# Which earlier readings an attention score group waits for, in a one-core hybrid decoder layer

## The chip, the core and the metric

The kernel runs on one core of a Trainium2 chip. The core has a matmul engine (PE, with its weight loads shown apart as PEld), a vector engine (DVE), a scalar engine (ACT), GpSimd (POOL), a queue engine that here mostly issues transfers (SP), and 16 DMA engines. Each engine carries out its own list of instructions in order; between engines they wait on semaphores. The metric is the device time of one launch in microseconds (us), lower is better. PE's clock is granted by a throttle; the profile gives it as a share of full speed.

## The reference

One decoder layer on x (1 x 2048 x 1024), float32. What matters here:

```
hn = rms_norm(h, mix_pre_g)
proj = hn @ w_in                      # q, k, v for attention and u for the convolution group
attn_out = sliding_window_attention(q, k, v, attn_sinks, rel_bias)
conv_out = conformer_conv(u, ...)     # GLU, causal depthwise conv of width 31, layer norm, swish, pointwise
mixed = concat([attn_out, conv_out]) @ w_out
h = h + rms_norm(mixed, mix_post_g)
hn = rms_norm(h, ffn_pre_g)
ff = (silu(hn @ w_gate) * (hn @ w_up)) @ w_down
h = h + rms_norm(ff, ffn_post_g)
```

Attention has 8 query heads of 64 in two groups that share a key and a value head each. In blocks of 128 queries, each query sees its own block of keys and the one before, inside a window of 128, with a bias by distance and one learned sink per head:

```
s = einsum("bnqhgd,bnkhd->bnhgqk", qb, kb) * scale
s = where(valid, s + bias, -inf)
m = maximum(max(s), sink);  p = exp(s - m)
p = p / (sum(p) + exp(sink - m))
o = einsum("bnhgqk,bnkhd->bnqhgd", p, vb)
```

The feed-forward width is 2816.

## The kernel before

**Stages.** The sequence is cut into four token tiles of 512 (t = 0 to 3). Every product is float32 in two parts, high and low, and so three matmuls; nearly all matmuls are issued by one helper (line 108 of the profile), so rows are told apart by tile names, whose letter after the @ is the stage. Stage A is the input projection of a tile (GLU units, then keys, values and queries), B its attention, C its convolution group (480 tap operations on DVE for the four tiles, `fc@C` at L85 in the profile, then transposes into the bank `ct`), W the output projection, H builds the operands of the feed-forward product (the layer uses sums and differences of them), F is gate and up, G the down projection. J joins the convolution group's pointwise product with the output projection; X is preparation.

**Interleaving.** Stages are Python generators. A main stage runs and "lanes" with other stages are pumped beside it by a model of the time that has gone by: B, C and W0 beside A, C and H0 and the rest of B beside W1 and the first part of F, C, W and H of the later tiles beside G. The instructions so emitted go to a scheduler (a tile framework with a timeline model, L1558), which sets every engine's final order by priority and by when it reckons an instruction ready. An added dependency can therefore change the order of all engines.

**PSUM banks.** There are eight: four `mm`, three `tr`, one `ct`. Attention works in the `tr` banks.

**Attention (stage_b).** It works on four blocks of 128 queries a tile. `front(b)` computes a block's scores in two groups. A group takes two `tr` banks and fills them with 12 matmuls, alternating between the banks (`tr@B<-kz,ql@A` in the profile). The matmuls after a group's first get a very high priority, so that a group is issued in one piece once its first is. DVE reads each bank: it masks (L469) and then, per head, adds the bias and takes the maximum while it writes the scores out (L472). The last reading of each bank is recorded in a list by `freed`: two entries per group. After both groups ACT takes the exponentials (L492). `back(b)` scales, transposes the probabilities of four heads into one `tr` bank (L514), copies them out on ACT (L515, recorded by `freed`), has GpSimd select the part that belongs to the block before (L517), twice; then eight matmuls (four in the first block of all) form the weighted sums in a `tr` bank (`tr@B<-p@B,vd@B` and `tr@B<-p@B,vtok`), ACT copies them to `at` (L544, recorded by `freed`), and a transfer on ACT's queue writes them to `mixT` in DRAM (L546). The order of emission in a tile is front 0, front 1, back 0, front 2, back 1, front 3, back 2, back 3.

**The order around a score group.** The first matmul of a group is tied by explicit, synchronizing dependencies to two entries of `freed`'s list: the third-last and the second-last. With three banks handed out in turn these are the last uses of the two banks that the group overwrites; the last entry is the use of the bank that it doesn't touch.

**Neighbours that the prediction speaks of.** Keys `kz` and values `vtok` are single buffers per tile. W0's and W1's operands are loaded from `mixT` on SP's queue (L765; `fa@W`, and `mb@J` for W1's first load), split by ACT (L754) and DVE, and multiplied into `mm` banks. The next piece of the convolution is loaded on SP's queue (L603, `fc@C<-y_scr`) and transposed at L575. H0 transposes columns into the one bank `ct` (L863); ACT scales them out into one of two `gb` buffers (L883), a transfer on ACT's queue stores these (L884).

Of the kernel before, what the change touches and what calls it, by code (L numbers as in the profile page):

```python
# [37 lines left out]
def layer_kernel(ctx, tc, x, xT, cols, rows, sinks, relb, onehot, w_in, w_pw, w_out, w_gate, w_up, w_down, out):  # L38
# [19 lines left out]
    def f4(tag, shape=(P, D)):  # L58
        return t_(tag, shape)
# [7 lines left out]
    def sm(n, dt=F32):  # L67
        kind = "A" if lab[0][0] == "G" else lab[0][0]
        return sb.tile([P, 8], dt, tag="sm" + kind, name=nm("sm"), bufs={"C": 8, "W": 4}.get(kind, 16))[:, 0:n]
# [37 lines left out]
    def mat(*args, **kw):  # L107
        r = nc.tensor.matmul(*args, **kw)  # L108
        if not inlane[0]:
            lead_pe[0] = r  # L110
        return r
# [68 lines left out]
    def after_first(first, r, how=mybir.DependencyClass.NoSync):  # L180
        tc.add_manual_dep(
            r.ins,
            first.ins.name,
            mybir.DependencyInfo(how, mybir.DependencyReason.DATA),
            reason="order",
        )
# [244 lines left out]
    done_ = []  # L431

    def stage_b(t):
# [3 lines left out]
        def freed(r):  # L437
            done_.append(r)

        def front(b):  # L440
            lab[0] = L
            first = t == 0 and b == 0
            tok = slice(b * P, (b + 1) * P)
            win = slice(b * P, b * P + 256)
            mx = sm(8)
            pr = f4("p", (P, 8, P))
            for ip in range(2):
                os = [tr().rearrange("p (j k) -> p j k", j=2) for _ in range(2)]
                lead = []
                pq = tc.cur_priority  # L450
                for j in range(2):
                    i = 2 * ip + j
                    for n, (a, k) in enumerate(((0, 0), (0, 1), (1, 0))):
                        for g in (1, 0):
                            sl = slice(64 * g, 64 * g + 64)
                            if lead:
                                tc.cur_priority = pq - 10000
                            r = mat(os[g][:, j], q[i][sl, a, tok], kz[sl, k, win], start=n == 0, stop=n == 2)
                            if lead:
                                after_first(lead[-1], r)  # L460
                            else:
                                for x_ in done_[-3:][:2]:
                                    after_first(x_, r, mybir.DependencyClass.Sync)
                            if len(lead) < 2:
                                lead.append(r)
                tc.cur_priority = pq + 1
                for g in range(2):
                    prev = neg.unsqueeze(2).to_broadcast([P, 2, P]) if first else os[g][:, :, 0:P]
                    nc.vector.copy_predicated(os[g][:, :, P:], upper.unsqueeze(1).to_broadcast([P, 2, P]), prev)  # L469
                    for j in range(2):  # L470
                        h = 4 * g + 2 * ip + j
                        read = nc.vector.tensor_tensor_reduce(  # L472
                            out=pr[:, h],
                            in0=os[g][:, j, P:],
                            in1=bias[0][:, h],
                            op0=ALU.add,
                            op1=ALU.max,
                            scale=1.0,
                            scalar=NEG,
                            accum_out=mx[:, h : h + 1],  # L480
                        )
                    freed(read)
                yield 1.3
                lab[0] = L
            negm = sm(8)
            stt(negm, mx, -1.0, nsnk, ALU.mult, ALU.min)
            es = sm(8)
            vtt(es, negm, snk, ALU.add)
            act(es, es, AF.Exp)
            den = sm(8)  # L490
            for h in range(8):
                act(pr[:, h], pr[:, h], AF.Exp, bias=negm[:, h : h + 1], accum_out=den[:, h : h + 1])  # L492
            vtt(den, den, es, ALU.add)
            rd = sm(8)
            nc.vector.reciprocal(rd, den)
            live[b] = pr, rd
            yield YC
# [54 lines left out]
        for b in range(5):  # L552
            if b < 4:
                yield from front(b)
            else:
                yield YC
            if b:
                yield from back(b - 1)
# [1004 lines left out]
```

## Time and profile before

| | us |
| --- | --- |
| median of three runs | 1950.12 (1946.66 to 1955.75) |
| the profiled execution's own time | 1951.89 |
| its span in the trace | 1950.2 |
| PE busy | 1903.6 (98%) |
| DVE busy | 1488.7 (76%) |
| ACT busy | 969.9 (50%) |
| POOL busy | 296.2 (15%) |
| mean granted clock of PE | 0.992 |

The span runs from the first to the last instruction of one profiled execution. A row of a timeline gives start, duration, engine, line, tiles, shapes and a count, and in square brackets the idle time ahead of it with what ended that; a row of the chain gives start and share of the time for which that step set the end; a row of waits gives total, number and longest.

### The profile page before, as it was taken

What the parts mean: (1) busy time and instruction counts of PE and PEld (TensorE: products, weight loads), DVE (VectorE), ACT (ScalarE), POOL (GpSimd) and SP (SyncE); (2) the same over time, 40 slices, a digit from 0 to 9 for tenths busy, and PEclk for the clock granted to TensorE, in tenths of its full rate; (3) what the DMA queues carried; (4) which work ended last, traced back from release to release, by engine and by line L of the source; (5) the groups of instructions that cost most, each with busy time, mean ns of one, the idle gap of its engine ahead of it and who ended that gap; (6) DMA issues with size and microseconds to landing.
All of it is one profiled execution on the core that took longest, in us unless ns stands there. A gap on an engine that the chain in (4) does not pass through costs nothing.

```text
span 1950.2 us, 26810 instructions
## 1 busy us (share of the span) xinstructions
PE 1903.6 (98%) x8730; PEld 1538.2 (79%) x8730; DVE 1488.7 (76%) x2707; ACT 969.9 (50%) x1910; POOL 296.2 (15%) x367
## 2 busy tenths in 40 slices
PE   9999999999899999999999999999999999999998
PEld 7877776777678878878878878877888888888886
DVE  5999899897775899888669985778766675455557
ACT  5356344657567533333364556576543433345443
POOL 6000101221012100000000010015332332311000
PEclk9999999999999999999999999999999999999999
DMA  8897646669668676877487688689644442375654
GB/s 317 276 320 236 224 158 195 195 217 342 226 221 276 231 240 220 265 258 259 134 306 247 216 295 276 203 310 352 226 153 165 162 157 97 130 249 184 215 190 156
DMA packets 229180, 443.55 MB, mean 227 GB/s; under 512 B 22920, under 2 KB 48688, under 8 KB 229040
## 3 DMA queue, kind: packets, MB, share of 16 engines
q1 hardware_dynamic: 207408, 406.19, 62.1%
q10 hardware_dynamic: 19392, 28.32, 4.0%
q0 software_dynamic: 2240, 7.34, 1.0%
q8 instruction: 68, 1.11, 0.2%
q14 instruction: 72, 0.59, 0.1%
HBM read 320.64 MB, written 121.12 MB: 227 GB/s over the span
## 4 chain that ended last, share of the span: by engine, by line
PE 65%; DVE 16%; DMA 12%; issue 3%; ACT 2%; POOL 2%; SPq 1%; DVEq 0%; ACTq 0%; POOLq 0%
PE mm@F L108 29%; PE mm@G L108 17%; PE mm@A L108 9%; DVE fc@C L85 5%; PE mm@W L108 4%; PE tr@W L108 2%; PE tr@B L108 2%; DMA raw@A<-w_in 2%; DVE w@F L85 2%; DVE mid@W L85 1%; PE ct@J L108 1%; DMA mixT<-fc@C 1%; DMA td<-fc@G 1%; DVE chl@F L85 1%; DVE hl@G L85 1%
## 5 line engine op out<-in xcount | busy, mean ns | idle before, releaser
L85 DVE SCALAR_TENSOR_TENSOR fc@C<-glu@C,colt,fc@C 128x512 f32<-128x512 f32 x480 | 353.4, 751 | 2.2
L108 PE MATMUL mm@F<-hl@H,w@F 128*128 128x512 f32 x1056 | 254.8, 390 | 0.3 <-ACT gb@F L1098 0.3
L108 PE MATMUL mm@G<-hl@G,hl@G 128*128 128x512 f32 x924 | 226.3, 395 | 4.6 <-DVE p@G L1225 1.7
L108 PEld LDWEIGHTS mm@F<-hl@H,w@F 128*128 128x128 f32 x1056 | 197.9, 188 | 41.7 <-ACT gb@F L1098 0.7
L108 PEld LDWEIGHTS mm@G<-hl@G,hl@G 128*128 128x128 f32 x924 | 172.3, 189 | 43.8 <-DVE hl@G L85 2.8
L108 PE MATMUL mm@A<-hl@A,w@A 128*128 128x512 f32 x840 | 204.0, 394 | 2.3 <-DVE hl@A L85 1.0
L108 PE MATMUL mm@G<-w@G,hl@G 128*128 128x512 f32 x876 | 199.5, 389 | 0.0
L845 ACT ACTIVATE w@F<-chl@F 128x512 fp32r<-128x512 f32 x220 | 135.3, 624 | 124.3 <-PE mm@F L108 114.2
L108 PEld LDWEIGHTS mm@G<-w@G,hl@G 128*128 128x128 f32 x876 | 164.5, 188 | 34.1
L108 PEld LDWEIGHTS mm@A<-hl@A,w@A 128*128 128x128 f32 x840 | 155.7, 188 | 40.5 <-issue 2.5
L85 DVE TENSOR_TENSOR w@F<-chl@F,w@F 128x512 fp32r<-128x512 f32 x198 | 144.7, 734 | 38.4 <-ACT w@F L845 38.2
L108 PE MATMUL mm@F<-mid@H,w@F 128*128 128x512 f32 x528 | 131.2, 391 | 2.1 <-ACT fa@F L1108 2.1
L108 PE MATMUL mm@F<-ql@H,w@F 128*128 128x512 f32 x528 | 130.8, 391 | 1.5 <-ACT w@F L845 1.5
L108 PE MATMUL mm@F<-p@H,w@F 128*128 128x512 f32 x528 | 129.1, 389 | 0.6 <-ACT at@F L1101 0.6
L108 PE MATMUL mm@F<-x@H,w@F 128*128 128x512 f32 x528 | 128.6, 391 | 0.1
L108 PEld LDWEIGHTS mm@F<-mid@H,w@F 128*128 128x128 f32 x528 | 99.2, 188 | 23.2 <-ACT fa@F L1108 2.5
L108 PEld LDWEIGHTS mm@F<-ql@H,w@F 128*128 128x128 f32 x528 | 98.7, 188 | 22.7 <-ACT w@F L845 1.9
L108 PEld LDWEIGHTS mm@F<-x@H,w@F 128*128 128x128 f32 x528 | 98.5, 188 | 22.4 <-issue 0.8
L108 PEld LDWEIGHTS mm@F<-p@H,w@F 128*128 128x128 f32 x528 | 99.0, 188 | 21.6 <-ACT at@F L1101 1.2
L133 ACT ACTIVATE w@A<-raw@A 128x512 fp32r<-128x512 f32 x110 | 67.5, 626 | 79.5 <-PE mm@A L108 46.1
L85 DVE TENSOR_TENSOR w@G<-raw@G,w@G 128x512 fp32r<-128x512 f32 x73 | 50.8, 696 | 68.5 <-ACT w@G L845 62.5
L108 PE MATMUL mm@W<-w@W,hl@W 128*128 128x512 f32 x384 | 99.9, 407 | 1.8 <-ACT hl@W L754 1.7
(308 smaller groups left out, 3253.9 us busy)
## 6 DMA issues: line engine op xcount, KB each, us to landing
mids<-fa@F SPq DMA_DIRECT2D x154, 256.0 KB, 2.6
raw@A<-w_in SPq DMA_DIRECT2D x55, 512.0 KB, 4.8
w@A<-lo_in SPq DMA_DIRECT2D x84, 256.0 KB, 3.7
fc@G<-mids SPq DMA_DIRECT2D x77, 256.0 KB, 3.4
fa@G<-mids SPq DMA_DIRECT2D x75, 256.0 KB, 5.1
w@W<-lo_out SPq DMA_DIRECT2D x48, 256.0 KB, 4.9
chl@F<-w_gate SPq DMA_DIRECT2D x22, 512.0 KB, 4.5
raw@F<-w_gate SPq DMA_DIRECT2D x22, 512.0 KB, 3.6
```

The lines of the kernel that those rows point to most:

```text
L85: r = op(*args, **kw)
L108: r = nc.tensor.matmul(*args, **kw)
L133: act(w[:, 0], raw, AF.Copy)
L845: act(w[:, 0], x, AF.Copy)
```

## The change

The first matmul of a score group is tied to the two latest entries of the list in place of the third- and second-last. Behind another score group these are the last readings of both of that group's banks. Behind a `back` they are the copy of the second transposes (L515) and the copy of the weighted sums (L544). The hazards of the banks themselves are kept by the framework in either case. No instruction of computation is added or taken away.

```
                             if lead:
                                 after_first(lead[-1], r)
                             else:
-                                for x_ in done_[-3:][:2]:
+                                for x_ in done_[-2:]:
                                     after_first(x_, r, mybir.DependencyClass.Sync)
                             if len(lead) < 2:
                                 lead.append(r)
```

More of the change, by code (lines that the diff above doesn't have):

```diff
@@ L461, in front @@
                             else:
-                                for x_ in done_[-3:][:2]:
+                                for x_ in done_[-2:]:
                                     after_first(x_, r, mybir.DependencyClass.Sync)
```

## The prediction

> **What bounds the kernel now.** I began with the page's busy shares, then read the chain that ended last in order of time.
>
> ```profile
> span 1950.2 us, 26810 instructions
> PE 1903.6 (98%) x8730; PEld 1538.2 (79%) x8730; DVE 1488.7 (76%) x2707; ACT 969.9 (50%) x1910; POOL 296.2 (15%) x367
> ```
>
> ```profile
> 1736.41 196.53 PE mm@G L108 x867
> ```
>
> The matmul engine is busy 98% of the span, and the last chain has stretches such as 867 matmuls back to back, 196.53 / 867 = 0.227 us each. The change touches no instruction, only the order, so this work stays. What can move is the 1950.2 − 1903.6 = 46.6 us in which PE is idle, and the stretches in which it was granted half its clock.
>
> Third, PE's waits in the whole span. The columns are total, times, longest:
>
> ```profile
> PE ct@H L863 <- ACT gb@H L883: 5.1, 3, 3.3
> PE tr@B L108 <- DVE sm@B L472: 3.2, 2, 2.9
> PE tr@B L108 <- POOL p@B L517: 2.8, 1, 2.8
> PE ct@C L575 <- DMA fc@C<-y_scr: 1.8, 1, 1.8
> PE mm@W L108 <- ACT hl@W L754: 1.7, 2, 1.3
> ```
>
> The second row is the score groups' own wait (for the readings at L472): 3.2 us of 1950. The instructions' timelines put nearly all of the first, second and fifth rows at two places, which I call spot 1 and spot 2. Spot 1, first PE's and SP's rows, then the chain:
>
> ```profile
> 324.24 0.97 PE L108 MATMUL tr@B<-kz,ql@A 64*128 64x256 f32 x12
> 332.40 1.55 PE L108 MATMUL tr@B<-kz,ql@A 64*128 64x256 f32 x12 [2.85 <-DVE sm@B L472]
> 335.23 0.80 PE L108 MATMUL mm@W<-w@W,hl@W 128*128 128x512 f32 x1 [1.28 <-ACT hl@W L754]
> ```
>
> ```profile
> 324.41 4.69 DMA mixT<-at@B
> 329.11 0.32 SPq L765
> 329.96 4.57 DMA fa@W<-mixT
> 334.55 0.64 ACT hl@W L754
> ```
>
> A block's second score group (332.40) waits for the readings of its first (324.24), which on DVE lie behind a run of convolution taps. Then W0's first matmul (335.23) waits for operands whose load sits on SP's queue behind W1's first load, and that one waits for the write of B1's last weighted sums (324.41 + 4.69 = 329.10). Spot 2, rows of PE, of ACT and of the chain:
>
> ```profile
> 519.18 0.97 PE L108 MATMUL tr@B<-kz,ql@A 64*128 64x256 f32 x12 [0.39 <-DVE sm@B L472]
> 524.05 1.11 PE L863 MATMUL ct@H<-ident,fa@H 128*128 128x128 f32 x4 [3.32 <-ACT gb@H L883]
> 523.32 0.69 ACT L883 ACTIVATE gb@H<-ct@H,colt 128x512 f32<-128x512 f32 x1 [4.21 <-DMA hT<-gb@H]
> 516.50 6.71 DMA hT<-gb@H
> ```
>
> H0's turned columns (L863) share the single bank ct; its reader at L883 writes one of two gb buffers and so waits for the 6.71 us write of the buffer two columns before. Last, stretches: length, busy of PE, PEld, DVE, ACT and POOL, granted clock, DMA share, GB/s:
>
> ```profile
> 325.00:345.00 20.00, 15.87 (x71) 12.59 (x70) 20.00 (x55) 6.33 (x11) 1.08 (x2) 0.83 0.68 212
> 332.50:339.40 6.90, 5.62 (x22) 4.46 (x23) 6.90 (x14) 1.83 (x4) 0.54 (x1) 0.51 0.87 277
> 345.00:393.00 48.00, 48.00 (x255) 37.71 (x254) 39.73 (x98) 30.44 (x75) 11.87 (x23) 1.00 0.65 201
> 500.00:526.00 26.00, 20.12 (x112) 14.74 (x111) 18.77 (x49) 14.83 (x38) 0.77 (x2) 0.96 0.72 233
> 523.70:530.50 6.80, 6.01 (x16) 4.54 (x17) 4.51 (x16) 5.29 (x16) 0.64 (x1) 0.50 0.48 152
> 526.00:576.00 50.00, 49.95 (x237) 37.10 (x237) 43.08 (x100) 34.59 (x85) 10.90 (x18) 0.95 0.52 174
> ```
>
> After each of the two long waits PE ran some 6.8 us at half its clock: 0.51 after spot 1's 2.85 us, 0.50 after spot 2's 3.32 us.
>
> **The added wait itself.** The first matmul of every score group now waits for the two latest readings of score banks instead of the last uses of just its own two banks; everything behind it in PE's order waits too. How late those readings are, from rows of PE, DVE and ACT:
>
> ```profile
> 180.95 0.97 PE L108 MATMUL tr@B<-kz,ql@A 64*128 64x256 f32 x12
> 176.57 0.09 DVE L472 DVE_READ_ACCUMULATOR2_ANT sm@B<- 128x1 f32 x1
> 114.84 0.97 PE L108 MATMUL tr@B<-kz,ql@A 64*128 64x256 f32 x12 [0.83 <-DVE sm@A L85]
> 114.19 0.07 DVE L472 DVE_READ_ACCUMULATOR2_ANT sm@B<- 128x1 f32 x1
> 114.62 0.07 DVE L472 DVE_READ_ACCUMULATOR2_ANT sm@B<- 128x1 f32 x1
> 165.12 0.97 PE L108 MATMUL tr@B<-kz,ql@A 64*128 64x256 f32 x12
> 166.13 0.58 ACT L544 ACTIVATE at@B<-tr@B 128x512 f32<-128x512 f32 x1
> ```
>
> Behind another score group the readings are long over: 4.3 us at 180.95, the common case. Only at 114.84 does the second bank's reading end 0.43 us after the first's (114.62 against 114.19), so +0.4 us there; a like group in B3 now stands close behind its forerunner, for which I take +1.1 us (0 to 2.85, the row at 332.40 being the longest such wait).
>
> Behind weighted sums it is different: at 165.12 the group started before the copy of the sums (166.13 to 166.71) had run, and in the old order at least eight groups stand directly behind the sums. Kept in that order the new wait would cost each up to 166.71 − 165.12 = 1.6 us, some 13 us in all. But the scheduler reorders: in the new order of PE's instructions 4 to 22 other matmuls stand between the sums and the group, 0.9 to 5 us at 0.227 us each. That is more than the copy's start and 0.58 us need after the sums' last matmul, about 0.7 us, so I cost it at 0; if projection matmuls were missing there, the price is the 13 us above. So much for the wait; what is left is the reordering, which runs over stages A, B, C, W and H of all token tiles.
>
> **Spot 1.** In the new order that second group stands 12.3 us of PE work behind its first instead of 4.1, and on SP's queue four of W0's loads (and a weight load) stand ahead of W1's first load. Both waits, 2.85 + 1.28 = 4.1 us, and the lost clock, (1 − 0.83) × 20.00 = 3.4 us, can go: 7.5 us. Late next is the load of the convolution's next piece, whose wait is the fourth row of PE's waits; the chain there:
>
> ```profile
> 392.50 0.61 DVE fc@C L85
> 393.50 5.11 DMA fc@C<-y_scr
> ```
>
> DVE's work ahead of that piece is only 1.1 us less in the new order. But from 345 to 393 DVE was idle 48.00 − 39.73 = 8.3 us, so it is no hard stop. Between 0 (DVE paces) and 7.5 I take a gain of half, 3.7, as the traced wait is neither gone nor the full bound.
>
> **Spot 2.** The waits are 5.1 (all three at ct are here), 0.39, and the other wait for hl@W, 1.7 − 1.28 = 0.4, which is W1's here: 5.9 us. The clock lost is (1 − 0.96) × 26.00 + (1 − 0.95) × 50.00 = 3.5 us. Together 9.4. In the new order the first column comes 5 us earlier and the score groups are spread between the other columns; the pitch set by two gb buffers and a 6.71 us write stays, so of 5.1 us about 3.3 us of waits should remain, in pieces too short to halve the clock. That frees 9.4 − 3.3 = 6.1 us; as the columns' readiness is a guess, I take two thirds, 4.1, between 0 and 9.4.
>
> [...]
>
> **The late part.** From 1120 to 1340 us (W2, W3 and H2 beside stage G and the next F) the order changes too. The waits that show there:
>
> ```profile
> PE mm@G L108 <- DVE p@G L1225: 1.7, 1, 1.7
> PE tr@H L863 <- issue: 1.5, 1, 1.5
> PE mm@G L108 <- DVE x@G L85: 1.4, 1, 1.4
> ```
>
> At best 4.6 us go, at worst as much comes; nothing says which, so 0, with ±4.6 for the range. Stages F and the end of G keep their order: 0.
>
> **The sum.** −3.7 − 4.1 + 0.4 + 1.1 = −6.3 us. The profiled execution took 1951.89 us (1.7 us outside its span), 1.8 above the median of 1950.12; so 1950.12 − 6.3 = 1943.8, called 1944.
>
> **The rivals.**
> No gain: PE reaches the next limit sooner and waits there. For it speak the wait at L575 and DVE's 20.00 busy of 20.00 us around spot 1; against it the 8.3 us that DVE idles before 393. Sum: +1.5 − 1.5, about 1950.
>
> Slower: a late GpSimd select. At two places the new order leaves fewer matmuls between a block's transposes and its weighted sums: 2.7 us of PE work instead of 6.6 in B1's second block, 3.6 instead of 6.1 at B1's end. The sums read what GpSimd selects at L517. The rows of POOL, DVE and PE where this already bit:
>
> ```profile
> 205.58 8.36 POOL L517 TENSOR_SCALAR_AFFINE_SELECT p@B<-p@B 128x512 f32<-128x512 f32 x2 [15.84 <-ACT p@B L515]
> 203.49 9.36 DVE L85 SCALAR_TENSOR_TENSOR fc@C<-glu@C,colt,fc@C 128x512 f32<-128x512 f32 x14
> 213.99 1.08 PE L108 MATMUL tr@B<-p@B,vd@B 128*64 128x512 f32 x4 [2.77 <-POOL p@B L517]
> ```
>
> Two selects took 8.36 us while a run of taps lasted on DVE, and PE waited 2.77 us. With 2.7 and 3.6 us of cover the same two selects would leave waits of 5.7 and 4.8 us, each with some 3.4 us of half clock behind it as after spot 1: 17 us, minus the 6.3: 1950 + 11 = 1961. [...] But DVE has gaps at most places (39.73 of 48.00 busy), and the 2.77 us wait was not followed by half clock, which speaks for a lower price.
>
> Both spots gone and nothing new: −7.5 − 9.4 + 1.5 = −15.4, about 1935; against it stands the gb pitch.
>
> **How the numbers follow.** Forecast 0.44 (own range 1938 to 1949: the spots at a third or at nearly full), no gain 0.22, late select 0.24, both spots gone 0.10. One measurement tells about 0.5%, 9.75 us, from no change (the three runs spread 9 us). Faster than 1940.4: all of the last case and a third of the forecast's, 0.24. Slower than 1959.9: most of the late selects and a little of no gain, 0.24. The rest 0.52. The range runs from the last case less part of the late stretch, 1933, to the late selects with one more microsecond, 1962; the tails outside, mainly several late selects or a lost cover behind the sums (+13), are about 2 in 10.
>
> **What would show it.** In the changed profile: PE's wait for sm@B at L472 falls from 3.2 us to 1.5 or less, mm@W's wait for hl@W from 1.7 towards 0, ct@H's wait for gb@H from 5.1 to about 3; no half clock around 330 and 525 us, so a mean clock above the 0.992 of before. No gain would show as a longer wait of ct@C for fc@C<-y_scr; the late select as waits of tr@B for p@B at L517 of 4 us or more. Waits of score matmuls for at@B at L544 would break the step on cover.

## The result and the profile after

The changed kernel took 1970.49 us (median of 6 runs, 1963.37 to 1977.87), the kernel before 1950.96 us in the same comparison: a ratio of 1.0096, 95% interval 1.0079 to 1.0113. It is slower by about 19 us, against a forecast of 6.3 us less. The profiled execution took 1970.99 us. Its page, first lines:

```profile
span 1969.3 us, 26817 instructions
PE 1910.3 (97%) x8730; PEld 1539.8 (78%) x8730; DVE 1486.7 (75%) x2707; ACT 972.5 (49%) x1912; POOL 299.4 (15%) x367
```

The number of matmuls is the same; the span grew by 19.1 us. PE's idle time grew from 46.6 to 59.0 us, and the same matmuls were busy for 6.7 us longer. The mean granted clock, 0.991 after 0.992, accounts for 2 to 3 us of these 6.7; where the rest comes from the record does not show. The longest of PE's waits in the changed kernel's whole span, and those that the prediction named (total, times, longest):

```profile
PE tr@W L108 <- DVE mid@W L85: 4.2, 1, 4.2
PE mm@F L108 <- ACT w@F L845: 3.7, 1, 3.7
PE tr@W L108 <- ACT ql@W L754: 3.6, 2, 3.1
PE tr@B L108 <- POOL p@B L517: 3.4, 2, 2.6
PE mm@G L108 <- ACT hl@G L845: 3.2, 1, 3.2
PE mm@A L108 <- DVE x@W L85: 3.2, 1, 3.2
PE mm@F L108 <- DVE fa@F L85: 2.9, 1, 2.9
PE mm@W L108 <- DVE ql@A L85: 2.4, 1, 2.4
PE tr@H L863 <- issue: 2.1, 1, 2.1
PE ct@C L575 <- DMA fc@C<-y_scr: 1.7, 2, 1.2
PE mm@W L108 <- ACT hl@W L754: 1.6, 2, 0.9
PE mm@F L108 <- ACT mm@F L999: 1.4, 1, 1.4
PE ct@H L863 <- ACT gb@H L883: 0.8, 1, 0.8
```

Two of the rows that the prediction wanted gone are gone or small: the score groups' wait for their readings (3.2 us before) is no longer there, ct's for gb went from 5.1 to 0.8. The third, mm@W's wait for hl@W, hardly moved: 1.6 us after 1.7. No wait of score matmuls for at@B (L544) has appeared. The clock at the two spots is whole again, as the stretches of the changed kernel show (length, busy of PE, PEld, DVE, ACT, POOL, granted clock, DMA share, GB/s):

```profile
325.00:345.00 20.00, 18.15 (x95) 13.38 (x94) 19.74 (x34) 10.10 (x19) 5.38 (x5) 1.00 0.85 277
500.00:526.00 26.00, 25.38 (x146) 18.92 (x145) 23.43 (x60) 14.66 (x37) 1.47 (x2) 1.00 0.68 224
526.00:576.00 50.00, 48.83 (x247) 37.07 (x248) 45.58 (x108) 34.41 (x81) 8.39 (x16) 1.00 0.63 211
1226.00:1246.00 20.00, 15.78 (x57) 12.46 (x56) 9.10 (x15) 6.80 (x12) 1.72 (x1) 0.83 0.84 268
```

But six waits of 1.4 to 4.2 us stand there that before did not have, and they have nothing to do with score groups: W0's sums on DVE at 385 us (x@W), a query split at 485 (ql@A), a reading and a sum of F at 578 and 657 (L999, fa@F), and in the late part W3 (mid@W) and G (hl@G). The last stretch quoted, with 15.78 of 20.00 us busy at a clock of 0.83, holds the mid@W wait. The rows w@F and ql@W stand in before too, with 1.5 and 2.8 us.

One more thing is new: ACT has two instructions more, 1912 after 1910. They are loads of a function table, 1.28 us each, at 571.80 (ahead of a block's eight exponentials, L492) and at 579.96 (ahead of a reading of F, L1003). The new order puts those exponentials among F's readings, and the wait for L999 at 578 us comes behind the first load and the exponentials.

Where the time came from can be read, roughly, off the start of the same matmul in both traces (worked out from the start times; difference to before in us):

```
                               first of F   first of G   386th of G   last of G
before, start                     543.3        984.1       1125.4       1940.2
changed kernel                     +0.4         +4.4         +6.5        +19.1
```

In this pair of traces all gains and losses before F cancel, 4 us come beside F, and 12.6 us come after 1125 us, in the late part. But each column is a single execution, and the early rows vary from one to the next. The changed kernel's trace is already 3.1 us behind at 37 us, where the two orders are still the same. The experiments e2 and e4 below have the same early order as the changed kernel, and their traces stand at +7.5 and +3.0 at the first matmul of F, and at +13.3 and +13.6 at the 386th of G. So the traces put the early part at 6.5 to 13.6 us, and what comes behind that matmul in the new late order at 9.4 (e2) to 12.6.

### The profile page after: what moved, and what is told of

Its sections match the earlier page's. It is cut to its first block, busy times and chain, and to the rows that moved or that the text cites. A ratio compares the mean times of both kernels' runs of the same rounds, so it can differ in the third digit from the quotient of the medians.

```text
span 1969.3 us, 26817 instructions
## 1 busy us (share of the span) xinstructions
PE 1910.3 (97%) x8730; PEld 1539.8 (78%) x8730; DVE 1486.7 (75%) x2707; ACT 972.5 (49%) x1912; POOL 299.4 (15%) x367
## 4 chain that ended last, share of the span: by engine, by line
PE 69%; DMA 11%; DVE 11%; issue 3%; ACT 3%; POOL 1%; SPq 1%; DVEq 0%; ACTq 0%; POOLq 0%
PE mm@F L108 29%; PE mm@G L108 17%; PE mm@A L108 12%; PE tr@W L108 3%; DVE fc@C L85 3%; PE mm@W L108 2%; PE tr@B L108 2%; DMA mixT<-fc@C 1%; DVE w@F L85 1%; DMA at@W<-mixT 1%; PE ct@J L108 1%; DVE mid@W L85 1%; DMA td<-fc@G 1%; DMA wx@G<-w_down 1%; DVE chl@F L85 1%
## 5 line engine op out<-in xcount | busy, mean ns | idle before, releaser
L845 ACT ACTIVATE w@F<-chl@F 128x512 fp32r<-128x512 f32 x220 | 135.1, 625 | 127.7 <-PE mm@F L108 117.7
L108 PE MATMUL tr@W<-w@W,ql@W 128*128 128x512 f32 x384 | 100.7, 404 | 7.8 <-DVE mid@W L85 4.2
```

The costliest lines, as they stand in the source:

```text
L845: act(w[:, 0], x, AF.Copy)
```

## The experiments

**Order or waits?** The kernels e1 to e4 (and later e5 to e8, e11 and e12) hold every engine to a given order. To the end of the program a function is added that ties each instruction to the one that precedes it in a list, by dependencies that order the issue on one engine and make nothing wait; the lists are the orders of the two programs. The cut between "early" and "late" lies in the middle of F, where on every engine the same instructions have gone before in both.

```
     with tile.TileContext(nc, schedule_with_timeline_sim=True) as tc:
         layer_kernel(tc, *aps, out)
+        keep_order(tc)
...
+            for a, b in zip(names, names[1:]):
+                tc.add_manual_dep(
+                    traced[b], a, mybir.DependencyInfo(mybir.DependencyClass.NoSync, mybir.DependencyReason.DATA),
```

The order of before with the new waits (line 462 as in the change):

> Every engine's instructions in the order of before, but with the two waits of the changed kernel. If the added waits themselves cost time where no matmul stands between the weighted sums and the next score group, as the prediction priced it (1.6 us at each of eight places): 1951 + 13 = about 1964 us. If the waits are nearly free even there (the copy is over by the time, or the lost time is given back at the next wait): 1950 to 1954 us.

The order of the changed kernel with line 462 as before:

> Every engine's instructions in the order of the changed kernel, but with the two waits of before. If the time is lost by the order alone: 1968 to 1973 us, as the changed kernel. If the waits themselves cost it: about 1951 to 1956 us.

Line 462 as before, old order early and new order late:

> Waits of before; on each engine the order of before up to the middle of the feed-forward stage F (about 900 us) and the order of the changed kernel from there on. If the new order of the late part (W2, W3, H2 beside G, 1120 to 1360 us) costs the bulk: +12 to +13 us, 1963 to 1964. If the early part with the score groups does: not over 1955.

Line 462 as changed, new order early and old order late:

> Waits of the changed kernel; on each engine its order up to the middle of stage F and the order of before from there on. If the late part costs the bulk: 1951 + 19 - 13 = about 1957 (two traces put the early part at 0 to +6). If the early part does: 1965 or more.

Measured against before: e1 1.0040 (1.0023 to 1.0057), e2 1.0100 (1.0084 to 1.0116), e3 1.0080 (1.0063 to 1.0096), e4 1.0054 (1.0037 to 1.0070). In e1's waits the new one shows, at just the eight places where no matmul covers it:

```profile
PE tr@B L108 <- ACT at@B L544: 7.6, 8, 2.7
```

Three things follow.

First, in the changed kernel the waits themselves cost nothing that shows: without them, in the same order, the time is the same (1.0100 against 1.0096, each to within 0.17%). Nor does holding the engines to an order show a cost: e7 below, which holds the order of before but for a few steps, measures 0.9999.

Second, where the waits are not covered they cost 7.6 us in eight waits by the trace and 0.0040 x 1954 = 7.8 us by the runs; neither "free" nor the priced 13. Seven of the eight are 0.70 to 0.72 us long. The eighth, at 387.82, is 2.67 us: there the copy of the sums stood on ACT behind a split that waited 2.58 us for W0's load.

Third, the whole loss is the order. The late part's order alone costs 0.0080 x 1954 = 15.6 us by the runs, somewhat over the 12 to 13 expected of it. The early part's costs 10.6, which lies between the two expectations of e4. The two together are 26 us, more than the 19 of the whole. Each of the three has an interval of 3.3 us either way; together (root of the sum of squares) that is 5.7 us, so some 2 us of the difference of 7 are not covered. The traces put the late part lower, at 11.8 us in e3, by the matmuls from the 386th of G on.

**What is late in the late part?** ACT's rows in the changed kernel's timeline:

```profile
1205.55 0.78 ACT L629 ACTIVATE fc@C<-ct@C,lnh 128x512 f32<-128x512 f32 x1 [1.17 <-PE ct@C L627]
1210.53 0.63 ACT L754 ACTIVATE ql@W<-at@W 128x512 fp32r<-128x512 f32 x1 [3.53 <-DMA at@W<-mixT]
1216.73 0.63 ACT L754 ACTIVATE ql@W<-at@W 128x512 fp32r<-128x512 f32 x1 [4.83 <-DMA at@W<-mixT]
1217.26 0.76 ACT L629 ACTIVATE fc@C<-ct@C,lnh 128x512 f32<-128x512 f32 x1
1235.63 0.63 ACT L754 ACTIVATE ql@W<-at@W 128x512 fp32r<-128x512 f32 x1 [4.93 <-DMA at@W<-mixT]
```

and in before's:

```profile
1197.76 0.77 ACT L629 ACTIVATE fc@C<-ct@C,lnh 128x512 f32<-128x512 f32 x1
1199.74 0.63 ACT L754 ACTIVATE ql@W<-at@W 128x512 fp32r<-128x512 f32 x1 [0.55 <-DMA at@W<-mixT]
1204.17 0.78 ACT L629 ACTIVATE fc@C<-ct@C,lnh 128x512 f32<-128x512 f32 x1 [3.80 <-DMA mixT<-fc@C]
1208.88 0.63 ACT L754 ACTIVATE ql@W<-at@W 128x512 fp32r<-128x512 f32 x1 [2.22 <-DMA at@W<-mixT]
1222.69 0.63 ACT L754 ACTIVATE ql@W<-at@W 128x512 fp32r<-128x512 f32 x1 [5.61 <-DMA at@W<-mixT]
```

C3's four pieces go one by one through ACT (L629), DVE, a write to `mixT` and a load back for W3 (L765), which ACT splits (L754). Before, the second piece is followed by one split and then the third piece's L629 (1204.17). In the new order two splits stand between them; the second waits 4.83 us for its load, and the third piece, whose transposes PE ran at 1211.30, comes behind it at 1217.26. The last split starts at 1235.63 in place of 1222.69, 12.9 us later, where PE had been 6.5 us late at 1125, and PE stands still for it (mid@W, 4.2 us), with a clock of 0.52 in the 7.00 us from 1237 to 1244. e5 moves just these steps in e3:

```
 ACT:  +third piece L629, L631    ahead of the second split of W3 (L754)
       +fourth piece L629, L631   ahead of W3's next weight split and G's splits
 DVE:  +third and fourth sum of C3, each ahead of the same steps
 SP:   +third write to mixT       ahead of a load of F's weights that waits
       +fourth write to mixT      right behind the load of W3's third operand
```

> The kernel of the late order (e3: 1.008 of before) with six steps moved: the evaluation of C3's third and fourth piece (tanh and scale on ACT, their sum on DVE, the write to mixT on SP) goes back ahead of W3's operand splits and of loads that wait, as it stands in before. If the late loss is that chain of pieces (PE's waits of 4.2 us for mid@W and the half clock behind it, 3.4 us): 7 us less than e3, about 1.004 of before. If the loss lies in the order at large and only shows up there: 1.007 to 1.008, the wait reappears elsewhere.

Measured 1.0037 (1.0022 to 1.0052), the number that the chain's expectation gives. The traces support less of it. Rows of PE's waits from 1125 to 1365 us, e3's

```profile
PE tr@W L108 <- DVE mid@W L85: 4.1, 1, 4.1
PE mm@G L108 <- ACT hl@G L845: 3.2, 1, 3.2
PE tr@H L863 <- issue: 2.1, 1, 2.1
```

became e5's

```profile
PE tr@W L108 <- DVE mid@W L85: 2.8, 2, 2.5
PE tr@H L863 <- issue: 2.1, 1, 2.1
PE mm@G L108 <- ACT hl@G L845: 1.3, 1, 1.3
```

The mid@W wait is smaller, not gone. PE's order is the same in e3 and e5, so the two traces can be set side by side matmul by matmul. Between 1179 and 1241 us, where the moved steps are, e5 gains 2.8 us, not 7: part of the mid@W wait and of the half clock behind it (the stretch 1226 to 1246 has a clock of 0.91 after 0.83). Another 3.5 us are gained at the hl@G wait and behind it. That wait stands at 1174 us, ahead of the first moved step (about 1206 us), so this gain is not the edit's; e2, with the changed kernel's order, has 1.3 us there too, and the changed kernel 3.2. By the runs the gain is 0.43%, some 8 us, with an uncertainty of 4.4. So the six steps are shown to matter; that they carry half of the late loss rests on the runs alone. The remaining 0.37%, the third row among it, was not taken apart.

**The two spots by themselves.** e6 and e7 keep the order of before and move only these:

```
e6  DVE: +mask and four readings of B2's first group (L469, L472)  ahead of six taps
    SP:  +W1's first load (mb@J, x2)                               behind W0's four loads
e7  PE:  +third column's transposes (ct@H)                         19 matmuls earlier
         +12 matmuls of W1                                         between the columns
    ACT: +third column's reading (L883, L884, L886)                ahead of two weight splits of F
    DVE: +two sums of W1                                           behind those matmuls
```

> The order of before with spot 1 mended by hand: the first group's mask and readings stand six taps earlier on DVE, and W1's first load stands behind W0's four loads on SP. By the prediction's step: -3.7 us (0 to -7.5), about 0.998 of before. By the rival of no gain (the next load, fc@C<-y_scr, waits instead): 0.9995 to 1.0005.

> The order of before with spot 2 mended by hand: the third column's transposes stand 19 matmuls earlier and its reading ahead of two weight splits on ACT, and 12 of W1's matmuls stand between the columns. By the prediction's step: -4.1 us (0 to -9.4), about 0.998 of before. If PE only waits later: 1.000.

e6 measured 0.9977 (0.9960 to 0.9995): −4.5 us (−7.8 to −1.0), the size of the forecast step. What is late next in e6 is another reading, not the load that the prediction named:

```profile
PE mm@W L108 <- ACT fa@A L355: 2.4, 1, 2.4
PE ct@C L575 <- DMA fc@C<-y_scr: 1.4, 1, 1.4
```

e7 measured 0.9999 (0.9985 to 1.0012). It did not mend the spot: F's two weight splits held up ACT, so the second score group waited 3.2 us for its readings. ACT's row:

```profile
519.51 1.32 ACT L845 ACTIVATE w@F<-raw@F 128x512 fp32r<-128x512 f32 x2 [4.65 <-PE mm@W L108]
```

The splits were released by W1's matmuls, not by their load, as the text of e11 has it: weights of W and of F are written to the same six buffers (`w`), and the 12 matmuls of W1 that e7 moved behind the sums hold theirs longer. e11 moves those two splits (ACT L845, and their low parts on DVE) behind the third column as well.

> As e7, with the two weight splits of F (they waited for their load and held back the second column's reading and the copy of the sums on ACT, and the readings on DVE) moved behind the third column. If spot 2 is worth what the prediction said (4.1 us, at most 9.4): 0.995 to 0.998 of before. If the pitch of columns through two gb buffers binds PE there whatever stands between: 0.999 to 1.001.

Measured 0.9995 (0.9979 to 1.0010). Counting the matmuls of `mm@W`, the 321st starts 0.9 us later than in before, the 353rd (531.6 us in before) 6.4 earlier, the last 1.5 earlier: 7.3 us are won in place and 4.9 lost again behind it, at a later column:

```profile
531.17 0.66 PE L863 MATMUL ct@H<-ident,fa@H 128*128 128x128 f32 x4 [3.01 <-ACT gb@H L883]
```

whose reading on ACT stands behind a block's eight exponentials and a weight split of F (526.26 to 530.45). The time measured is the one that e11's second expectation gives, but its mechanism is not shown: spot 2 can be mended in place, though by moving a few steps it was not turned into time. What it is worth alone stays open.

**The early part's loss.** e8 moves four steps in the kernel of e4:

```
 DVE: +two sums of W0 (x@W)        ahead of a split that waits for W0's load    (385 us)
 ACT: +split of the last query     ahead of W0's norm, which waits              (485 us)
 ACT: +reading of F (L995, L999)   ahead of four of a block's exponentials      (578 us)
 DVE: +sum of F (fa@F)             ahead of a weight split                      (657 us)
```

> The kernel of the early order (e4: 1.0054 of before) with four steps moved ahead of one that waits on the same engine: two sums of W0 on DVE (PE waited 3.2 us at 385), one query split on ACT (2.4 to 3.6 us at 485), one reading of F on ACT (1.4 to 2.6 us at 578), one sum of F on DVE (2.5 to 2.9 us at 657). If the early loss is these four queues: 9 to 12 us less than e4, 0.999 to 1.001 of before. If it is spread over the whole order: 1.003 to 1.005.

Measured 1.0021 (1.0004 to 1.0038): 0.33% or about 6 us less than e4, where 9 to 12 were expected, so between the two expectations. The four waits, 3.1, 3.6, 2.6 and 2.5 us in e4, are gone, and part of them came back elsewhere; e8's waits from 90 to 700 us begin

```profile
PE ct@C L575 <- DMA fc@C<-y_scr: 3.8, 3, 2.2
PE tr@B L108 <- POOL p@B L517: 3.4, 2, 2.6
PE mm@W L108 <- ACT mid@W L727: 3.1, 1, 3.1
```

of which e4 had only 1.3 us for the first, the same 3.4 for the second and none of the third.

**One tile at a time.** The new rule for one token tile, the old one for the others, with the scheduler free again (for tile 2; the others alike):

```
-                                for x_ in done_[-3:][:2]:
+                                for x_ in (done_[-2:] if t == 2 else done_[-3:][:2]):
```

> The new rule for the score groups of token tile 2 alone (spot 1 lies there), the old one for the others; the scheduler sets the order, and the late part (W2, W3, H2 beside G) keeps that of before. If each tile's new order brings its own sums: spot 1's gain (4.5 us in e6) less the two waits that stood at 385 and 485 us in the early order (5 to 7 us): 1.000 to 1.002 of before. If the new rule is good in itself and only the late part was unlucky: 0.996 to 0.998.

> The new rule for token tile 3 alone; PE's order differs only from spot 2's last column to the start of F, the late part is that of before. The columns before it stand as in before, so most of spot 2 stays; the new waits at 578, 612 and 657 us (4 to 6 us in the early order) should come: 1.001 to 1.003 of before. If they were due to the tiles before: 0.998 to 1.000.

> The new rule for token tile 0 alone. The late part keeps the order of before. If the early loss (e4: 1.0054) comes from single tiles, it has to come from tiles 0 and 1, as tiles 2 and 3 alone gave 0.9998 and 0.9988: 1.003 here or in tile 1. If it comes from their orders meeting: 0.999 to 1.001 in both.

> The new rule for token tile 1 alone, as in e13: 1.003 or more if this tile carries the early loss, 0.999 to 1.001 if none alone does.

Measured: tile 0 1.0007 (0.9993 to 1.0021), tile 1 0.9976 (0.9960 to 0.9992), tile 2 0.9998 (0.9983 to 1.0013), tile 3 0.9988 (0.9975 to 1.0000). The late part keeps the order of before in all four. Tile 2 lies just outside its first expectation; the second, that the rule is good in itself, would have been faster. Tile 3 falls on the side of its second expectation, though two waits for F's readings (L999, 3.7 us together) and the two table loads came in it as well, so these alone don't make a slower kernel. Tiles 0 and 1 do not carry the loss; tile 1 is even faster than either of its expectations. The sum of the four is −0.31%, 6 us less; the same rule in all tiles, with the same late order, is +0.54% (e4). So the rule in no single tile brings the early loss. Which combination of tiles does was not tested. Nor are the four runs slices of e4: a rule in one tile already reorders the tiles behind it, so each is an order of its own. Tile 1's version is, with e6, the fastest of the study, which nothing had forecast. Both spots are whole in it:

```profile
325.00:345.00 20.00, 18.86 (x101) 13.91 (x100) 19.26 (x45) 10.58 (x20) 3.25 (x4) 1.00 0.86 285
500.00:526.00 26.00, 25.52 (x154) 19.79 (x154) 24.86 (x67) 18.92 (x44) 5.39 (x4) 1.00 0.72 214
526.00:576.00 50.00, 49.39 (x241) 36.78 (x240) 42.57 (x90) 34.64 (x85) 9.00 (x16) 1.00 0.66 227
```

though the rule was not applied in the tiles of the spots: a waiting group in tile 1 shifts the modelled time, and the order of tiles 2 and 3 follows.

e12 took the order of e10, e6's two moves, and one reading of A (L355) ahead of an operand split on ACT:

> The order of e10 (new rule in tile 3 alone, 0.9988 of before) with spot 1 mended as in e6 (0.9977) and one reading of A (fa@A, for which PE waited 2.4 us in e6) moved ahead of an operand split on ACT. If the two gains add: 0.9965, with the third 0.995. If later waits take them: 0.998.

Measured 0.9988 (0.9975 to 1.0001): the two gains do not add. Its wait for fc@C<-y_scr is 2.8 us, the limit that the prediction's rival of no gain named, and two waits in F are 4.5 us together (mm@F for L999; 3.7 in e10).

## Why the prediction was wrong

**The added wait itself: right.** Costed at 0 where other matmuls cover it; e2 shows it, and the wait for at@B (L544), named as the sign against it, is not in the changed kernel's list. The price without cover was too high: 1.6 us was taken for each place, and the waits are 0.7 us at seven of the eight places, 0.95 in the mean. The small costs of +0.4 at B0 and +1.1 at B3 did not come.

**Spot 1 and spot 2: right in kind, for the most part.** The long waits fell (2.85, 1.28 and 5.1 us to 0, 0.68 and 0.8; the last was to stay at about 3.3) and the clock at both spots came back (1.00 from 325 to 345 and from 500 to 576 us). Short waits at ct left the clock whole: 0.78 us at 526.27 in the changed kernel, 0.78 and 0.95 us at 516.52 and 518.13 in before, where the clock is 1.00 from 500.00 to 523.70. Two signs failed: W1's wait for hl@W at spot 2 grew from 0.4 to 0.9, so that row as a whole went from 1.7 to 1.6 and not towards 0, and the mean clock is 0.991, not above 0.992, as the clock fell at other places (0.52 from 1237 to 1244 us, 0.70 from 657 to 662). Spot 1 alone is worth 4.5 us against the forecast 3.7; spot 2's worth alone is open. That the two gave their 7.8 us in the changed kernel can't be read from its trace: at the first matmul of F it stands at +0.4.

**The failed step is "The late part": "nothing says which, so 0, with ±4.6 for the range".** Its order costs 15.6 us by itself by the runs of e3, 9.4 to 12.6 by the traces: at least twice the bound. The bound was wrong in kind. I took the waits that stand in that stretch of before as the size of what a new order could bring; they bound only what it can take away. What the runs show in its place is a chain from engine to engine and through DRAM: ACT, DVE, SP, write, load, ACT, for four pieces, on queues where one step put ahead holds up the next piece while it waits for its own load (4.83 us at 1216.73). Moving six steps of this chain back took 0.43% of the 0.80% away (e5). Which chains make the rest is open, and that the length of such chains bounds the loss is argued, not measured.

**The second failed step is the sum.** It has terms for two places of a reordering that ran from 110 to 640 us, and silently 0 for all others. Four of the other places cost 1.4 to 3.2 us each in the trace, and moving the steps behind them (e8) took back about 6 of the 10.6 us; the early part as a whole is +0.54% where −0.3% was forecast. What brings the rest of the early loss stays open. That the forecast equals the sum of the four tiles taken alone (−0.31%) is chance and no confirmation: the kernel has the rule in all of them.

**The rivals.** The late GpSimd select did not decide: PE's wait at L517 is 3.4 us against 2.8, with 0.8 at the second place. No gain by the next load: that wait is 1.7 against 1.8. The kernel did end slower, and beyond the 1961 us of the slower rival, but by another mechanism than any rival had.

## What to carry to other kernels

Where a scheduler sets the order, a changed dependency can reorder the whole program behind it; it is not an edit at one place. Price each stage whose order changes by the chains that run through it, and do not take the waits that stand there now as a bound on the loss. Before judging such an edit, hold the order and change the waits, then hold the waits and change the order; here that took two kernels and told that the added waits were harmless in the order that came with them. And keep what a few moved instructions give (0.9977) apart from what a rule gives: the rule for one tile gave as much, the rule for all lost 1%. Last, before two traces are compared at one place, look how far apart they are where nothing differs yet: here up to 3 us.

## What the runs showed of the hardware

Behind waits of nearly the same length PE ran at its full clock in one execution (1.00 behind 3.18 us) and at half in another (0.50 behind 3.16 us). In the changed kernel, the 3.18 us before 384.78 and what followed (length, busy of PE, PEld, DVE, ACT, POOL, granted clock, DMA share, GB/s):

```profile
381.60:384.78 3.18, 0.01 (x1) 0.00 (x0) 1.34 (x3) 1.81 (x3) 0.00 (x0) 1.00 0.98 366
384.78:388.00 3.22, 3.22 (x14) 2.68 (x15) 3.22 (x8) 2.81 (x11) 0.56 (x1) 1.00 0.24 90
```

and the same place in e4, which has the same early order:

```profile
380.80:383.96 3.16, 0.06 (x2) 0.01 (x1) 1.35 (x3) 1.81 (x3) 0.00 (x0) 0.87 0.98 366
383.96:389.50 5.54, 5.54 (x13) 4.38 (x14) 5.47 (x12) 5.13 (x21) 1.20 (x3) 0.50 0.55 177
```

The stretch of 5.54 us at a clock of 0.50 costs some 2.8 us (an estimate, 5.54 x 0.50), so these two executions differ by about that at this place. In before the waits of 2.85 us (332.40) and 3.32 us (524.05) had a clock of 0.51 and 0.50 behind them, the one of 2.77 us (213.99) had 1.00:

```profile
211.20:213.99 2.79, 0.02 (x1) 0.00 (x0) 1.65 (x3) 0.01 (x1) 2.74 (x2) 1.00 0.57 176
213.99:217.00 3.01, 3.01 (x21) 1.49 (x22) 0.76 (x2) 0.60 (x1) 0.00 (x0) 1.00 0.00 0
```

So the length of a wait alone does not tell here whether the clock falls behind it; what else decides it these runs do not show.
